# Six o tiles, weight buffers over both attention halves, and h differences made with h, in a windowed-attention encoder layer

## The chip, the cores and the metric

The kernel runs on one core of a Trainium2 chip. The metric is the time of one execution on the device, in microseconds (us). The core has five engines that run their own instruction queues in order: PE (TensorE, the matrix products), DVE (VectorE), ACT (ScalarE), POOL (GpSimd) and SP (SyncE, which here only issues DMAs). They wait for each other by semaphores.

## The reference

One layer of an encoder: windowed grouped-query attention, then a SwiGLU feed-forward, each between two RMSNorms with adaLN shift, scale and gate taken from a conditioning vector c. There are 2048 tokens of width 1024, 16 query heads over 4 key/value heads of width 64, a hidden width of 2816, all in fp32.

```
c_act = silu(c)
mod = c_act @ ada_w + ada_b                       # 6 x 1024
sh1, sc1, g1, sh2, sc2, g2 = split(mod, 6)
h = rmsnorm(x, mix_norm_pre) * (1 + sc1) + sh1
y = windowed_gqa_sink(h, w_qkv, w_o, sink, bias)  # blocks of 128 queries against 384 keys
x = x + g1 * rmsnorm(y, mix_norm_post)
h = rmsnorm(x, ffn_norm_pre) * (1 + sc2) + sh2
y = (silu(h @ w_in_a) * (h @ w_in_b)) @ w_out
x = x + g2 * rmsnorm(y, ffn_norm_post)
```

## The kernel before

**Products.** Every large product is done as three matmuls (`three`, L144 to L148): each operand is split into a high and a low part (`split`, L150 to L152: ACT casts the high part, DVE or POOL subtracts it to get the low part), and hi*hi, hi*lo and lo*hi are summed in one PSUM bank. A tile of 128x512 results over 1024 inputs takes 24 matmuls of 512 columns.

**Chunks and units.** The 2048 tokens are four chunks c of 512. Chunks 0 and 1 get their q, k and v first. Then 64 attention units follow, one for each chunk, key/value head g and block of 128 queries. A unit (L408) is named by its block b = 4c+jb and by g: `s8_0_3` is the score product of block 8, key/value head 0, fourth query head. A unit has eight score matmuls (L430), a DVE reduction with the bias (L435), exponentials on ACT (L437), a scaling on POOL (L443); two units later come its transposes (`t`, L453), their split, the products with v (`o`, L458 and L459) and the store of the result to `o_d` (L467).

**Fillers.** Between two units `Budget.pull` lets a generator write a few matmuls of other work into PE's queue: 19 a unit in the first 32 units, 20 in the second (`FILL`). In the first half these are q, k and v of chunks 2 and 3 (tiles `psq2_n`, `psq3_n`, 24 tiles of 24 matmuls). In the second half they are the output projection (`OProj`, L515): eight tiles `py{c}_{n}` a chunk, each from the four attention results `ol{c}_{g}` (L526, split by POOL, for chunk 3 by DVE) and a weight tile `wo{c}_{n}` (for chunks 0 and 3 loaded raw as `wor` at L537 and split; chunk 0 writes its split weights to `wo_d`, chunks 1 and 2 load them, L542). The last six `py` tiles of chunk 2 are held until the scores of the last unit are queued. `psF`, two PSUM banks, is shared by the `py` tiles and by the small sums `nst` of the norms.

**Ends.** `ends` (L569) follows a chunk's `py` tiles: the sum of squares `nsto` (two matmuls), the residual x1 on POOL (L505, L506, stored to `x1_d`), the second sum `nstx`, and `make_h2` (L497 to L500: a POOL multiplication, an ACT scale and shift, a store to `h2_d`). Chunk 1's `make_h2` comes last of these, after the final attention units. Chunk 3's projection (`py3_n`) follows by itself, with its own pools. For chunks 2 and 3 norm, residual and h are made later, inside the feed-forward (`late_residuals`, one step per block).

**Feed-forward.** It works on halves hf of 1024 tokens. A block (L731) forms two by two output tiles from seven products of sums and differences of operands, 84 matmuls of 512 columns (`pc0_u` to `pc6_u`). The token operands are h of two chunks (`b11`, `b21`, `b22`) and four differences (`t1` to `t4`); the seven weight operands are made and split by DVE for each block (`ws`, `wa`, L752 to L760). For hf 0 the h tiles are loaded back from `h2_d` as `fx` (L881), 12 for `b11` and `t2` and 16 for the rest; the differences are made on the spot: DVE at L887 and L888, and in `differences` POOL at L705 and L710 and DVE at L706 and L712. For hf 1 they are loaded ready-made from `hd_d`.

**adaLN.** The 48 columns `mod` are 48 DVE reductions of a 128x1024 weight tile `ada` against the broadcast silu(c) (L260), spread over the projection and attention phases; tiles 40 to 47 give the gate g2, used only in the last norm.

**Order.** The program is written in one order and a scheduler sorts each engine's queue by its own model when it is built; the queues are fixed from then on. Buffers come from pools stacked from the left or the right end of the on-chip memory: a pool opened in the place of an older one waits for the last use of the tiles that lay there.

## Time and profile before

| what | us |
|---|---|
| median of 3 runs (lowest to highest) | 2191.41 (2188.45 to 2195.57) |
| the profiled execution | 2197.15 |
| its span in the profile | 2195.3 |
| busy in it: PE / DVE / ACT / POOL | 2072.1 / 1668.4 / 1080.6 / 774.2 |

The profile is of one execution. A row of the page's groups reads: line, engine, operation, the tile written and those read, shape, count, then busy time and mean nanoseconds of one, and last how long the engine had idled just before these instructions and which engine, tile and line ended that. A row of the table of windows gives for a stretch of time each engine's busy time and number of instructions, PE's granted clock as a share of the full one, and the DMA engines' share and rate. A busy PE is not always a fast one, since a matmul that runs at a lower clock counts as busy for longer; the number of matmuls in a window tells more.

### The profile page before, as it was taken

How to read it: one execution, taken by the hardware profiler on the slowest of the kernel's cores; microseconds unless marked ns; L12 is line 12 of the kernel's file. 1: busy time of each engine (PE TensorE's matmuls, PEld its weight loads, DVE VectorE, ACT ScalarE, POOL GpSimd, SP SyncE). 2: the span in 40 equal slices, each digit the busy share in tenths (PEclk: the TensorE clock that was granted, in tenths of full speed). 3: DMA queues.
4: the chain of work that ended last, by engine and by line, in shares of the span. 5: the costliest groups of instructions: out<-in, count | busy, mean ns of one | idle time of the engine just before them, and what ended most of it. 6: DMA issues, size and time to landing. Idle time of an engine off the chain costs nothing. (4 is left out here: it accounts for less than half of the span.)

```text
span 2195.3 us, 28935 instructions
## 1 busy us (share of the span) xinstructions
PE 2072.1 (94%) x9366; PEld 1677.9 (76%) x9366; DVE 1668.4 (76%) x2917; ACT 1080.6 (49%) x2125; POOL 774.2 (35%) x695
## 2 busy tenths in 40 slices
PE   6998999989989998899999989999999999998997
PEld 4786878767777776778888868888888788877886
DVE  8657676676766579877888797766664788999987
ACT  4546565677757664443434353333332654465432
POOL 3403333355696865434344522222221000220040
PEclk8998999999999999999999999999999999999998
DMA  8786665576865683444445663223231544348442
GB/s 287 252 272 225 189 195 166 167 232 213 301 222 204 202 311 129 152 163 153 161 156 180 220 226 110 107 101 115 101 105 41 205 149 148 127 152 278 158 130 101
DMA packets 195764, 390.05 MB, mean 178 GB/s; under 512 B 19563, under 2 KB 61596, under 8 KB 190492
## 3 DMA queue, kind: packets, MB, share of 16 engines
q1 hardware_dynamic: 195036, 387.68, 53.0%
q8 instruction: 74, 1.21, 0.2%
q14 instruction: 78, 0.64, 0.1%
q10 hardware_dynamic: 576, 0.52, 0.1%
HBM read 268.55 MB, written 119.57 MB: 177 GB/s over the span
## 5 line engine op out<-in xcount | busy, mean ns | idle before, releaser
L435 DVE CUSTOM_DVE_ANT_0 pr<-s,bias,nsink 128x384 f32<-128x384 f32 (+1 forms) x256 | 149.1, 595 | 121.6 <-PE s L430 100.0
L147 PE MATMUL pc_i<-ht,ws_i 128*128 128x512 f32 x528 | 207.2, 392 | 1.0 <-DVE ht L152 1.0
L146 PE MATMUL pc_i<-ht,ws_i 128*128 128x512 f32 x528 | 207.5, 393 | 0.6 <-DVE u_i L813 0.6
L148 PE MATMUL pc_i<-ht,ws_i 128*128 128x512 f32 x528 | 207.0, 392 | 0.0
L823 POOL TENSOR_TENSOR p_i<-p_i,u_i 128x512 f32<-128x512 f32 x44 | 80.0, 1818 | 326.8 <-DVE u_i L810 180.9
L437 ACT ACTIVATE pr<-pr,nm 128x385 f32<-128x385 f32 (+1 forms) x256 | 154.0, 605 | 72.3 <-DVE nm L435 64.2
L958 POOL TENSOR_TENSOR z<-z,z 128x512 f32<-128x512 f32 x32 | 53.8, 1696 | 358.6 <-DVE z L954 338.4
L443 POOL TENSOR_SCALAR pr<-pr,rs 128x384 f32<-128x384 f32 (+1 forms) x256 | 146.3, 591 | 92.4 <-DVE rs L441 90.5
L430 PE MATMUL s<-k,q 128*128 128x384 f32 (+1 forms) x512 | 138.9, 368 | 23.4 <-DVE nm L435 15.7
L151 ACT CAST ws_i<-s_i 128x512 fp32r<-128x512 f32 x132 | 81.5, 619 | 128.4 <-PE pc_i L148 122.3
L146 PE MATMUL pc_i<-hb,wa_i 128*128 128x512 f32 x352 | 139.3, 396 | 0.6 <-DVE b_i L807 0.6
L151 ACT CAST wa_i<-wiri 128x512 fp32r<-128x512 f32 x132 | 81.9, 620 | 117.2 <-PE pc_i L148 111.1
L148 PE MATMUL pc_i<-hb,wa_i 128*128 128x512 f32 x352 | 138.9, 395 | 0.0
L147 PE MATMUL pc_i<-hb,wa_i 128*128 128x512 f32 x352 | 138.8, 394 | 0.0
L152 DVE TENSOR_TENSOR plo<-t,phi 128x512 fp32r<-128x512 f32 x184 | 121.7, 683 | 13.2 <-ACT phi L151 12.3
L430 PEld LDWEIGHTS s<-k,q 128*128 128x128 f32 x512 | 89.7, 200 | 46.8 <-DVE nm L435 29.9
L146 PEld LDWEIGHTS pc_i<-ht,ws_i 128*128 128x128 f32 x528 | 99.3, 188 | 24.4 <-issue 1.0
L147 PEld LDWEIGHTS pc_i<-ht,ws_i 128*128 128x128 f32 x528 | 99.2, 188 | 23.7 <-DVE ht L152 1.5
L453 PE MATMUL t<-ident,pr 128*128 128x128 f32 x736 | 114.0, 281 | 2.5 <-DVE plo L152 2.3
L148 PEld LDWEIGHTS pc_i<-ht,ws_i 128*128 128x128 f32 x528 | 99.2, 188 | 22.2
L152 DVE TENSOR_TENSOR ws_i<-s_i,ws_i 128x512 fp32r<-128x512 f32 x132 | 107.7, 816 | 5.0 <-ACT ws_i L151 4.7
L152 DVE TENSOR_TENSOR wa_i<-wiri,wa_i 128x512 fp32r<-128x512 f32 x132 | 106.1, 804 | 5.6 <-ACT wa_i L151 5.3
(323 smaller groups left out, 6200.3 us busy)
## 6 DMA issues: line engine op xcount, KB each, us to landing
wiri<-w_in SPq DMA_DIRECT2D x88, 512.0 KB, 4.7
ada<-ada_w SPq DMA_DIRECT2D x48, 512.0 KB, 5.5
wiro<-w_out SPq DMA_DIRECT2D x48, 384.0 KB, 3.8
q_d<-e SPq DMA_DIRECT2D x64, 256.0 KB, 4.1
q<-q_d SPq DMA_DIRECT2D x16, 1024.0 KB, 5.5
wo<-wo_d SPq DMA_DIRECT2D x16, 1024.0 KB, 6.0
g_d_b<-p_i SPq DMA_DIRECT2D x44, 256.0 KB, 4.8
g_d_t<-p_i SPq DMA_DIRECT2D x40, 256.0 KB, 2.0
```

The costliest lines, as they stand in the source:

```text
L146: pe.matmul(ps, w[0], h[0], start=first, stop=False)
L147: pe.matmul(ps, w[0], h[1], start=False, stop=False)
L148: pe.matmul(ps, w[1], h[0], start=False, stop=last)
L151: act.copy(hi, src)
L152: return eng.tensor_tensor(lo, src, f(hi), ALU.subtract).ins
L430: m = pe.matmul(ps[:, :n], q[:, h, jb * P:(jb + 1) * P], kk[:, i, (jb + j0) * P:(jb + j1) * P], start=i == 0, stop=i == 1)
L435: red = dve.tensor_tensor_reduce(pr[:, h, :n], ps[:, :n], bias[g][:, h, j0 * P:j1 * P], -1.0, nsink[:, hh:hh + 1], ALU.add, ALU.min, nm[:, ...
L437: act.activation(pr[:, h, :n + 1], pr[:, h, :n + 1], AF.Exp, bias=nm[:, h:h + 1], scale=-1.0, accum_out=rs[:, h:h + 1])
L443: pool.tensor_scalar(pr[:, h, :n], pr[:, h, :n], rs[:, h:h + 1], 1.0, ALU.mult, ALU.mult)
L453: pe.transpose(pt[:, h * P:(h + 1) * P], pr[:, h, jj * P:(jj + 1) * P], ident)
L823: pool.tensor_tensor(sa, sa, b, ALU.mult)
L958: (pool if (i, x) in ((2, 2), (4, 4), (5, 5), (6, 6)) else dve).tensor_tensor(sums[hf, n2, x], sums[hf, n2, x], sums[hf, n2, y], ALU.add)
```

## The change

It has five parts.

1. **Fillers**: 18 instead of 19 matmuls a unit in the first half.
2. **Pools**: the x tiles `xs` and the norm's scratch `nrm` now lie at the bottom of their stack, below the h tiles. The projection's attention results get six buffers instead of four, opened where `xs` lay. The weight pool `ws` of the first half stays open and serves the projection's weights too, with two split buffers instead of three and two raw ones instead of one for chunk 0; the y tiles get 12 buffers instead of 14.
3. **adaLN**: tiles 40 to 47 leave the second half of attention, with the second copy of silu(c). They are done in the feed-forward as 16 reductions of half the width (`late_ada`), one per block after the late residuals, into hf 1.
4. **Chunk 1's h**: made in pairs of tiles. With each pair the two tiles of chunk 0's h are loaded back (`hf`), and the differences t1 to t4 are made by DVE and stored to a second `hd_d`. The residual's filler steps are four tiles each instead of three.
5. **Feed-forward start**: all 28 operands are loaded ready from `h2_d` and `hd_d` into their final place and only split there; the 16 DVE and 8 POOL differences on `fx` are gone.

```diff
@@ -44,12 +44,14 @@
-FILL = (19, 20)
+FILL = (18, 20)
-ADA_UNITS = (range(1, 32, 2), range(34, 52, 2))
+ADA_UNITS = range(1, 32, 2)
+OBUFS = 6
@@ -153,10 +156,10 @@
+    xs = open_pool(com, "xs", 8)
+    nrm = open_pool(com, "nrm")
     hs = open_pool(com, "hs", 2 * KT)
     ev = open_pool(com, "ev", 2)
-    nrm = open_pool(com, "nrm")
-    xs = open_pool(com, "xs", 8)
@@ -373,7 +375,7 @@
-    ws = open_pool(com, "ws", 2)
+    wop = ws = open_pool(att, "ws", 2, side="right")
@@ -512,6 +514,20 @@
+    def differences(b11, b12, b21, b22, give, engs=(pool, dve)):
...
@@ -523,7 +539,7 @@
-                t = op.tile([P, 2, 2, CH], F32R, tag="o", name=f"ol{c}_{g}", bufs=4)
+                t = op.tile([P, 2, 2, CH], F32R, tag="o", name=f"ol{c}_{g}", bufs=4 if c == NCH - 1 else OBUFS)
@@ -531,9 +547,9 @@
-                w = wop.tile([P, 2, KT, P], F32R, tag="w", name=f"wo{c}_{n}", bufs=2 if c == NCH - 1 else 3)
+                w = wop.tile([P, 2, KT, P], F32R, tag="w", name=f"wo{c}_{n}", bufs=2)
-                    raw = wop.tile([P, KT, P], F32, tag="raw", name=f"wor{c}_{n}", bufs=3 if c else 1)
+                    raw = wop.tile([P, KT, P], F32, tag="raw", name=f"wor{c}_{n}", bufs=3 if c else 2)
@@ -550,7 +566,7 @@
-                y = yp.tile([P, CH], F32, tag="y", name=f"y{c}_{n}", bufs=4 if c == NCH - 1 else 14)
+                y = yp.tile([P, CH], F32, tag="y", name=f"y{c}_{n}", bufs=4 if c == NCH - 1 else 12)
@@ -580,14 +596,19 @@
             for k in range(KT):
                 residual(c, k, self.ys[k], yp.tile([P, CH], F32, tag="xr", name=f"xr{c}_{k}", bufs=3), r,
-                if k % 3 == 2:
+                if k % 4 == 3:
-            yield
             for k in range(KT):
                 make_h2(self.ys[k], c, k, r)
-                if k % 3 == 2:
+                if k % 2:
+                    if c == CPH - 1:
+                        first = [yp.tile([P, CH], F32, tag="xr", name=f"hf{j}", bufs=3) for j in (k - 1, k)]
+                        for j in range(2):
+                            sp.dma_start(first[j], h2_d[c - 1][:, k - 1 + j, :])
+                        differences(first[0], self.ys[k - 1], first[1], self.ys[k],
+                                    lambda n, t: sp.dma_start(hd_d[0][k // 2][n], t) if n[0] == "t" else None, (dve, dve))
@@ -620,30 +641,23 @@
-    ada_units = [*ADA_UNITS[0], *ADA_UNITS[1]]
-    HALF_ADA = len(ADA_UNITS[0]) - 1
-    late = list(range(2 * KT + ADA_A, 6 * KT))
+    late = list(range(2 * KT + ADA_A, 5 * KT))
-    op = wop = yp = None
+    op = yp = None
         if i == half:
-            assert not waiting
+            assert not waiting and not late
             dve.tensor_tensor(coef[:, 1, :], mod[:, 16:24], gains[:, 1, :], ALU.mult)
             com.close()
+            op = open_pool(oend, "op", OBUFS)
-            cb = yp.tile([P, D], F32, tag="cb", name="cb2")
-            sp.dma_start(cb, cb_d)
-            cbs.append(cb)
-            wop = open_pool(oend, "wop", 2)
-            op = open_pool(oend, "op", 4)
@@ -653,11 +667,11 @@
-        if i in ada_units:
+        if i in ADA_UNITS:
-            waiting = [ada_load(late.pop(0), ws if i < half else yp)] if i != ada_units[HALF_ADA] and late else []
+            waiting = [ada_load(late.pop(0), ws)] if late else []
@@ -665,8 +679,6 @@
-    assert not late and not waiting
-    dve.tensor_tensor(coef[:, 3, :], mod[:, 40:48], gains[:, 3, :], ALU.mult)
@@ -686,31 +698,14 @@
+    wi = [open_pool(early, "wi0"), None]
     hA = open_pool(early, "hA", KT // 2)
-    wi = [open_pool(early, "wi0"), None]
...
@@ -864,51 +856,47 @@
-                                lambda n, t: sp.dma_start(hd_d[k // 2][n], t) if n[0] == "t" else None)
+                                lambda n, t: sp.dma_start(hd_d[1][k // 2][n], t) if n[0] == "t" else None)
-    late = late_residuals()
+    def late_ada():
+        for i in range(2):
+            cols = slice(i * CH, (i + 1) * CH)
+            cb = temp(f"cb{i}", "r", 2)
+            sp.dma_start(cb, cb_d[:, cols])
+            for t in range(5 * KT, 6 * KT):
+                w = temp(f"ada{t}_{i}", "r", 2)
+                sp.dma_start(w, a["ada_w"][t][:, cols])
+                yield
+                dve.tensor_tensor_reduce(w, w, cb, 1.0, (mod if i else adab)[:, t:t + 1], ALU.mult, ALU.add, mod[:, t:t + 1])
+        dve.tensor_tensor(coef[:, 3, :], mod[:, 40:48], gains[:, 3, :], ALU.mult)
+    late = chain(late_residuals(), late_ada())
-    st0 = ExitStack()
-    tmp0 = open_pool(st0, "tmp0", 10)
-    half = Operands("0", K2, None)
-    def h_blocks(k, names, st):
-        b = []
-        for n in names:
-            b.append(temp0(f"fx{k}_{n}_{st}"))
-            sp.dma_start(b[-1], h2_d[int(n[2]) - 1][:, 2 * k + (n[1] == "2"), :])
-        return b
+    half = Operands("0", K2, lambda n, k: hd_d[0][k][n] if n[0] == "t" else
+                    h2_d[int(n[2]) - 1][:, 2 * k + (n[1] == "2"), :])
     with tc.high_priority(offset=1):
-        for k in range(K2):
-            b11, t1, t2 = h_blocks(k, ("b11", "b12", "b22"), 0)
-            dve.tensor_tensor(t1, t1, b11, ALU.subtract)
-            dve.tensor_tensor(t2, t2, t1, ALU.subtract)
-            half.put("b11", k, b11)
-            half.put("t2", k, t2)
+        half.load("b11", "t2")
     lasto.close()
     wi[1] = open_pool(ffn, "wi1", side="right")
     with tc.high_priority(offset=100):
-        for k in range(K2):
-            differences(*h_blocks(k, ("b11", "b12", "b21", "b22"), 1),
-                        lambda n, t: half.put(n, k, t) if n not in ("b11", "t2") else None)
-    st0.close()
+        half.load(*[n for n in OPERANDS if n not in ("b11", "t2")])
     for hf in range(S // HALF):
                 hid.step(i)
-            if hf == 0:
-                next(late, None)
+            next(late, None)
-            half = Operands("1", K2, lambda n, k: hd_d[k][n] if n[0] == "t" else
+            half = Operands("1", K2, lambda n, k: hd_d[1][k][n] if n[0] == "t" else
+    assert next(late, None) is None
         hid.step(i)
```

The number of PE instructions is the same. On DVE the differences are 16 again, in another place, and eight reductions become 16 of half width; POOL has eight instructions fewer, the differences it made on `fx`. SP issues 33 more DMAs: eight loads `hf`, 16 stores to the second `hd_d`, eight more half `ada` loads, one for silu(c).

How the queues move, at the three places that the prediction speaks of. First PE where the second half of attention starts. Before, from the third score product of block 11, head 0:

```order
L459 MATMUL o7_3_5060<-plo7_3_2_5089,v1_3_4174 128x512
L453 MATMUL t8_0_2_5185<-ident_343,pr8_0_4907 128x128 x4
L430 MATMUL s11_0_1_5241<-k2_0_4577,q2_0_4575 128x384 x2
L146 MATMUL py0_0_5009<-ol0_0_4986,wo0_0_5003 128x512
L147 MATMUL py0_0_5009<-ol0_0_4986,wo0_0_5003 128x512
```

After, at the same tile `py0_0`:

```order
L432 MATMUL s8_0_3_4936<-k2_0_4546,q2_0_4544 128x384 x2
L455 MATMUL t7_3_0_5071<-ident_359,pr7_3_4812 128x128
L455 MATMUL t7_3_1_5082<-ident_359,pr7_3_4812 128x128
L149 MATMUL py0_0_5019<-ol0_0_4996,wo0_0_5013 128x512
L149 MATMUL py0_1_5122<-ol0_0_4996,wo0_1_5116 128x512
```

The first projection tile stands behind the scores of block 8 instead of block 11, three units earlier; the q, k, v tiles, which before ended two units before the half, now reach into its last unit.

Second, PE between chunk 1's projection tiles, where no filler is queued. Before (the rows left out are of the same units):

```order
L146 MATMUL py1_4_6526<-ol1_0_5941,wo1_4_6524 128x512
...
L430 MATMUL s15_0_0_6969<-k3_0_6202,q3_0_6200 128x256 x2
L430 MATMUL s12_1_0_7090<-k3_1_6683,q3_1_6681 128x384 x2
L430 MATMUL s13_1_0_7207<-k3_1_6683,q3_1_6681 128x384 x2
L430 MATMUL s14_1_0_7309<-k3_1_6683,q3_1_6681 128x384 x2
L128 MATMUL nstx0_6626<-nhix0_6627,ones_342 128x512
L146 MATMUL py1_5_6642<-ol1_0_5941,wo1_5_6640 128x512
```

After:

```order
L149 MATMUL py1_3_6415<-ol1_3_5952,wo1_3_6413 128x512
...
L432 MATMUL s10_3_0_6438<-k2_3_5776,q2_3_5774 128x384 x2
L432 MATMUL s11_3_0_6548<-k2_3_5776,q2_3_5774 128x384 x2
L432 MATMUL s12_0_0_6652<-k3_0_6198,q3_0_6196 128x384 x2
L432 MATMUL s13_0_0_6764<-k3_0_6198,q3_0_6196 128x384 x2
L432 MATMUL s14_0_0_6851<-k3_0_6198,q3_0_6196 128x384 x2
L432 MATMUL s15_0_0_6955<-k3_0_6198,q3_0_6196 128x256 x2
L131 MATMUL nstx0_6515<-nhix0_6516,ones_358 128x512
L149 MATMUL py1_4_6531<-ol1_0_5940,wo1_4_6529 128x512
```

The stretch without fillers, which ends behind `nstx0` in both, was four units long and is six now. Between `py2_1` and `py2_2`, where chunk 2's tiles are held, six units go without fillers in both.

Third, SP before the last projection `py3`. Before:

```order
L467 DMA o_d3_3_123<-of14_3_8037 256x1x128
L527 DMA ol3_0_8347<-o_d3_0_120 128x1024
L527 DMA ol3_1_8351<-o_d3_1_121 128x1024
L527 DMA ol3_2_8355<-o_d3_2_122 128x1024
L537 DMA wor3_0_8365<-w_o 128x1024
L467 DMA o_d3_3_123<-of15_3_8066 256x1x128
L563 DMA y_d0_324<-y2_5_8228 128x512
L537 DMA wor3_1_8399<-w_o 128x1024
L537 DMA wor3_2_8435<-w_o 128x1024
L500 DMA h2_d1_321<-y1_0_6057 128x512
L527 DMA ol3_3_8359<-o_d3_3_123 128x1024
```

After:

```order
L502 DMA h2_d1_337<-y1_3_6509 128x512
L543 DMA ol3_0_8380<-o_d3_0_120 128x1024
L558 DMA wo2_7_8307<-wo_d7_351 128x2048
L469 DMA o_d3_3_123<-of15_3_8060 256x1x128
...
L502 DMA h2_d1_337<-y1_7_7023 128x512
L579 DMA y_d0_340<-y2_6_8283 128x512
L543 DMA ol3_1_8384<-o_d3_1_121 128x1024
L543 DMA ol3_2_8388<-o_d3_2_122 128x1024
L553 DMA wor3_0_8398<-w_o 128x1024
L543 DMA ol3_3_8392<-o_d3_3_123 128x1024
```

The loads of chunk 3's first three attention results and of its first weight tile stood ahead of the stores of chunk 1's h; now three of the four and the weight stand behind all eight of these stores and behind the store of `y2_6`, and the last weight tile of chunk 2 behind the fourth of them. On DVE, after, twelve of the sixteen differences stand among the splits of `ol3`: the seven rows ahead of the last splits that `py3_0` needs are

```order
L521 TENSOR_TENSOR hf4_8295<-y1_4_6625,hf4_8295 128x512
L522 TENSOR_TENSOR y1_4_6625<-y1_5_6740,y1_4_6625 128x512
L526 TENSOR_TENSOR y1_5_6740<-y1_5_6740,hf4_8295 128x512
L155 TENSOR_TENSOR ol3_1_8384<-ol3_1_8384 128x1024
L155 TENSOR_TENSOR ol3_2_8388<-ol3_2_8388 128x1024
L155 TENSOR_TENSOR wo3_0_8397<-wor3_0_8398,wo3_0_8397 128x1024
L155 TENSOR_TENSOR ol3_3_8392<-ol3_3_8392 128x1024
```

so the difference of the sixth tile of chunk 1's h (`y1_5`) comes ahead of them, where before no row of h stood there.

33 lines of the change are left out of this document (14 added, 19 removed).

## The prediction

> **What bounds the kernel now.** I read the page's head and the chain that ended last, then the table of windows around the places the change touches, then PE's groups in the stretches where it loses time.
>
> ```profile
> span 2195.3 us, 28935 instructions
> PE 2072.1 (94%) x9366; PEld 1677.9 (76%) x9366; DVE 1668.4 (76%) x2917; ACT 1080.6 (49%) x2125; POOL 774.2 (35%) x695
> PE 36%; DVE 4%; DMA 2%; issue 1%; ACT 1%; POOL 0%; SPq 0%; DVEq 0%; POOLq 0%; ACTq 0%
> ...
> 484.00:584.00 100.00, 94.81 (x473) 77.07 (x474) 67.15 (x170) 68.33 (x158) 58.31 (x74) 0.98 0.73 251
> 735.00:786.00 51.00, 46.90 (x220) 37.72 (x219) 27.10 (x45) 33.89 (x70) 38.34 (x38) 0.97 0.76 237
> 786.00:814.00 28.00, 27.00 (x118) 21.98 (x118) 19.99 (x23) 19.89 (x31) 18.23 (x9) 1.00 1.04 383
> 814.00:838.00 24.00, 22.84 (x100) 18.56 (x100) 23.92 (x29) 14.11 (x26) 16.98 (x6) 1.00 0.47 166
> 838.00:862.00 24.00, 17.20 (x63) 12.32 (x62) 23.70 (x28) 12.02 (x22) 11.66 (x8) 0.93 0.34 109
> 862.00:880.00 18.00, 17.02 (x74) 13.40 (x72) 17.20 (x30) 8.05 (x14) 8.67 (x1) 1.00 0.35 132
> 1265.00:1310.00 45.00, 39.35 (x162) 30.35 (x161) 44.98 (x67) 25.62 (x48) 10.04 (x6) 0.96 0.69 248
> 1310.00:1700.00 390.00, 390.00 (x1690) 318.13 (x1690) 261.78 (x379) 118.53 (x198) 88.75 (x59) 1.00 0.27 96
> ```
>
> PE is busy 94% of the span and carries most of the chain. The change leaves its instructions alone, so it can only win back time in which PE waits or runs slowly. The last row gives PE's pace with nothing in its way: 1690 matmuls of 512 columns in 390 us, 0.231 us each, DVE at two thirds. In 814 to 862, where chunk 3's projection ends and the first feed-forward block runs, DVE is busy 47.6 of 48 us, while PE gets through 63 matmuls in the last 24 us instead of some 104. There DVE is the bound. Attention is of a third kind: nobody is full, and PE loses time unit by unit.
>
> **Attention.** PE's groups in 450 to 488, which ends where the projection has properly begun, then in 632 to 662 between chunk 1's projection tiles, and a row that prices transposes:
>
> ```profile
> L430 PE MATMUL s<-k,q 128*128 128x384 f32 x56 | 16.3, 383 | 4.2 <-DVE nm L435 3.9
> L453 PE MATMUL t<-ident,pr 128*128 128x128 f32 x68 | 12.0, 292 | 0.1
> L458 PE MATMUL o<-phi,v 128*128 128x512 f32 x17 | 7.5, 441 | 1.1 <-ACT phi L151 0.8 <-issue 0.2
> L459 PE MATMUL o<-plo,v 128*128 128x512 f32 x16 | 7.3, 456 | 0.2 <-DVE plo L152 0.2
> ...
> L453 PE MATMUL t<-ident,pr 128*128 128x128 f32 x52 | 8.9, 285 | 0.1
> L430 PE MATMUL s<-k,q 128*128 128x384 f32 x26 | 7.4, 392 | 5.7 <-DVE nm L435 5.7
> L459 PE MATMUL o<-plo,v 128*128 128x512 f32 x12 | 5.8, 480 | 0.0
> L458 PE MATMUL o<-phi,v 128*128 128x512 f32 x12 | 5.7, 478 | 0.4 <-DVE of L466 0.2
> L430 PE MATMUL s<-k,q 128*128 128x256 f32 x8 | 2.5, 438 | 0.3 <-DVE nm L435 0.3
> ...
> 481.42 0.60 PE L453 MATMUL t<-ident,pr 128*128 128x128 f32 x4
> ```
>
> Four transposes in a row end 0.60 us after the first began, one alone takes 0.28: 0.107 us each. By columns a score matmul of 384 is 0.173. The first stretch holds 56 x 0.173 + 68 x 0.107 + 33 x 0.231 (and three filler matmuls, 0.7) = 25.3 us of work in 38: 12.7 lost in seven units (56 scores by eight), 1.8 each. The second holds 17.9 us (six further matmuls among it) in 30: 12.1 lost in 4.25 units, 2.85 each. In 484 to 584 fillers are dense: a unit of 26 matmuls is 4.05 us of work, 20 fillers 4.62; 473 matmuls are 10.3 such units, 89 us of work in 100, 1.05 lost a unit. So a unit without fillers costs 0.75 to 1.8 us more than one with them.
>
> The number of fillers is fixed; early ones are missing later. In the first half 576 filler matmuls at 18 instead of 19 a unit last 32 units instead of 30.3: 1.7 units gained. In the second half the order puts `py0_0` three units earlier, the gap behind `nstx0` is two longer, the one ahead of `py2_2` unchanged: one unit. Together 2.7 units, 2.0 to 4.9 us. From the other side: if the 12.7 all went and two units at 2.85 came back, 7.0. Below, nothing: PE's queue is in order, and an early `py0_0` whose `ol` or `wo` is still in POOL's split holds up the scores behind it. I take **-4.5**. The nine `ada` reductions that leave (1.28 us each, row below) lay where DVE was busy 67 of 100: nothing.
>
> **The tail of attention.** The rows are PE's timeline, POOL's multiplications for chunk 1's h, and what the last projection must wait for: landing times, then casts and splits.
>
> ```profile
> 769.07 0.39 PE L129 MATMUL nstx<-nlox,ones 128*128 128x512 f32 x1
> ...
> 769.99 0.39 PE L148 MATMUL py<-ol,wo 128*128 128x512 f32 x1
> 773.24 0.50 PE L146 MATMUL py<-ol,wo 128*128 128x512 f32 x1 [2.87 <-ACT ysq L560]
> ...
> 785.67 0.39 PE L148 MATMUL py<-ol,wo 128*128 128x512 f32 x1
> 786.51 0.50 PE L146 MATMUL py<-ol,wo 128*128 128x512 f32 x1 [0.45 <-ACT ysq L560]
> ...
> L498 POOL TENSOR_TENSOR y<-y,nx x8: 1292/2224/2282, 775.6 to 789.2; 128x512 f32<-128x512 f32 x8
> ...
> wo<-wo_d SPq DMA_DIRECT2D x16, 1024.0 KB, 6.0
> ...
> ol<-o_d SPq DMA_DIRECT2D x4, 512.0 KB, 4.7
> ...
> L152 DVE TENSOR_TENSOR wo<-wor,wo 128x1024 fp32r<-128x1024 f32 x8 | 12.5, 1558 | 2.1 <-ACT wo L151 2.0
> L152 DVE TENSOR_TENSOR ol<-ol 128x1024 fp32r<-128x1024 f32 x4 | 7.5, 1905 | 4.2 <-ACT ol L151 4.2
> L151 ACT CAST wo<-wor 128x1024 fp32r<-128x1024 f32 x16 | 16.7, 1044 | 8.8 <-DMA wor<-w_o 8.7
> ```
>
> What may go: the pause before `py2_6` (773.24 less 770.22, 3.0) and its slow start, since two tiles took 12.7 us instead of 11.1 (1.6): -4.6. `py3_0` then followed with 0.45 us of idling.
>
> What comes: `wo2_7` is issued behind the store of `y1_3`. POOL's first multiplication began 6.5 us after `nstx1`; four of them at 1.29 to 2.28, about 1 for ACT and 6.0 to land make 18.7 to 22.6, and the turn of `py2_7`, three tiles after `nstx1` in the new order, is at 16.6: a wait of 2 to 6, I take +3. The loads of `ol3_1`, `ol3_2`, `wor3_0` and `ol3_3` stand behind the store of `y2_6`: 0.7 after `py2_6` for its copy (estimated as a 128x512 cast), some 1.5 for four issues, 4.7 to land, 1.0 to cast, 1.9 for the last split, 9.8 in all, against 5.5 of `py2_7` and its wait: 1.3 to 4.3, and 1.6 for a slow start as above. I take +5.5. Sum **+4**. Lower end: -4.6, if no load is late. Upper end: 24 stores and loads of 256 KB are new here, 6.3 MB, and
>
> ```profile
> DMA packets 7814, 17.17 MB, mean 264 GB/s; under 512 B 797, under 2 KB 2077, under 8 KB 7426
> ```
>
> is the rate in 735 to 800: 24 us if all of it went ahead of those loads. I stay near the lower half, because the order issues only about half of it ahead, and spread over three tiles.
>
> **The feed-forward's start.** The differences on `fx`, who waited for them, and block 1:
>
> ```profile
> L887 DVE TENSOR_TENSOR fx_b<-fx_b,fx_b x4: 678/686/1769, 791.5 to 806.4; 128x512 f32<-128x512 f32 x4
> L888 DVE TENSOR_TENSOR fx_b<-fx_b,fx_b x4: 678/686/694, 794.5 to 809.3; 128x512 f32<-128x512 f32 x4
> L706 DVE TENSOR_TENSOR fx_b<-fx_b,fx_b x4: 678/680/684, 824.9 to 852.2; 128x512 f32<-128x512 f32 x4
> L712 DVE TENSOR_TENSOR fx_b<-fx_b,fx_b x4: 679/1212/1772, 842.5 to 855.7; 128x512 f32<-128x512 f32 x4
> ...
> ACT ht L151 <- DVE fx_b L712: 9.0, 4, 4.1
> ...
> 884.97 0.80 PE L146 MATMUL pc_i<-hb,ws_i 128*128 128x512 f32 x1 [5.95 <-ACT p_i L794]
> ...
> L260 DVE CUSTOM_DVE_ANT_0 ada<-ada,cb,adab x48: 1272/1280/3514, 13.8 to 628.3; 128x1024 f32<-128x1024 f32 x48
> ```
>
> From 786 to 862 PE does 281 matmuls, 64.9 us of work in 76: 11.1 lost. The 16 differences cost DVE about 14 us there (four each at 0.95, 0.69, 0.68, 1.22), and the chain POOL, DVE, POOL, DVE made ACT wait 9.0 in front of the `t4` casts. Both leave. DVE's 67.6 us in these windows become 53.5, under PE's 64.9, and the number of loads (28) stays. At most 11.1 comes back; nothing, if splits of `ol3` and `wo3`, later now by the wait above, slide into it. I take **-8**. Block 1 lost 0.9 in 862 to 880 (18.0 less 74 x 0.231) and then 5.95 behind the same overfull DVE: **-4** of 6.8, between 0 and that.
>
> **adaLN later.** A half reduction is 0.64 us by the last row. Five stand, in the new order, ahead of hf 1's last operand splits, where DVE has no idle time (1265 to 1310: 44.98 of 45): 3.2 us. Eight weight operations of a later block, which stood there before, stand behind: I take 0, between -3 and +3.2. The eleven others fall into DVE's third of idle time (1310 to 1700); without that cover they would cost 7.
>
> **Sum**: -4.5 + 4 - 8 - 4 = -12.5, so 2197.15 becomes 2184.65 for an execution like the profiled one. That one lies 5.74 above the median of the runs shown; on the median's scale 2178.9, **2179 us**.
>
> **The rivals.**
> *More gain* (0.12): no load late at the tail, all that is lost is won. -7 - 4.6 - 11 - 6.8 = -29, 2162. For it: `py3_0` was nearly on time before. Against: the queue of SP.
> *The gain is eaten* (0.24): fillers only change places (0), both tail waits at their long ends (+10), block 0 gets half of its gain back (-6), block 1 -4. Zero, 2191; with two thirds of the waits 2188. For it: a fixed number of fillers.
> *Slower* (0.15), by one mechanism: DVE and POOL hold each other up. The fx rows have 0.68 and 1.77 us for one operation, POOL's row 1.29 and 2.28. Sixteen differences at 1.77 are 28 us instead of 11, while POOL multiplies `y1` at 2.28; `y1_5` comes 6.5 + 13.7 + 1 after `nstx1`, its two differences 3.5 later, and the four splits ahead of `py3_0` (7.3) behind those in DVE's queue: 32 us, against four tiles, 22.2. That is +9.8 and 1.6 of slow start instead of the +5.5, and 17 us more for DVE eat both feed-forward terms: -4.5 - 4.6 + 3 + 11.4 = +5.3; with another 2 for later `wo3` splits, 2199. It decides once the pairs really alternate; in the old trace only some did. The Trainium skill, "SBUF — State Buffer" (Who interferes with whom), has this as a rule: a DVE instruction with two inputs in SBUF and a GpSimd instruction that reads SBUF exclude each other, and the later one blocks until the first is through. By that rule moving differences beside POOL's multiplications would always cost; the trace agrees with the slow values, but its means lie in between, so it gets 0.15.
> *The reductions at hf 1's start cost* (0.07): all 3.2 and a DVE backlog for two blocks, +6, 2185.
>
> **How the numbers follow.** The forecast keeps 0.42, with a range of its own of 2172 to 2186. A measurement of this kernel can tell about 0.3%, 6.6 us, from no change, so faster means under 2184.8. The forecast gives 0.37 to faster, more gain 0.12, the two middle rivals 0.08: 0.57. No change: 0.05 + 0.2 + 0.03 = 0.28. Slower: 0.15. The range, from just above "more gain" to just under "slower", is 2163 to 2197.
>
> **What would show it.** Right: PE's matmuls dense from the scores of block 8 on; the stretch behind `nstx0` about 5 us per unit for six units; 786 to 862's DVE under 90% with no `fx` rows, and the first block's end 8 us closer to `py3_0`. A gap ahead of `py3_0`, released by DVE's `ol` split, of 2 to 6 us. Wrong: `y1` differences near 1.77 us, a gap there above 10, or PE idle at `py0_0` and `py0_1` behind POOL's splits.

## The result

| | us, median (lowest to highest) |
|---|---|
| before | 2191.05 (2188.45 to 2195.57), 4 runs |
| changed | 2166.02 (2165.77 to 2166.94), 4 runs |
| ratio | 0.9884, 95% interval 0.9867 to 0.9901 |

The change takes 25.0 us off, where my sum had 12.5. The four runs lie within 1.2 us; the four of before span 7, and 23 on a later chip 14.5 (2183.74 to 2198.26).

The head of the changed kernel's page, and its windows from the start of the second half of attention on. The edges: 463 `s8_0_0`, 715 `s15_3_0`, 774 `py3_0`, 860 the end of block 1, 1250 a place within the last two blocks of hf 0 (they begin at 1218), 1299 block 2 of hf 1.

```profile
span 2164.3 us, 28995 instructions
PE 2055.8 (95%) x9366; PEld 1666.6 (77%) x9366; DVE 1649.8 (76%) x2933; ACT 1076.4 (50%) x2125; POOL 737.5 (34%) x687
...
715.00:774.00 59.00, 47.53 (x221) 38.03 (x220) 32.05 (x56) 35.45 (x65) 32.80 (x34) 0.94 0.69 233
774.00:821.00 47.00, 46.81 (x192) 38.03 (x193) 35.26 (x46) 28.50 (x47) 13.27 (x6) 0.93 0.96 349
821.00:860.00 39.00, 39.00 (x171) 31.90 (x170) 37.93 (x56) 26.93 (x44) 13.90 (x7) 1.00 0.56 192
860.00:1250.00 390.00, 384.30 (x1658) 312.36 (x1657) 316.98 (x425) 155.95 (x261) 163.77 (x109) 0.99 0.54 180
1250.00:1299.00 49.00, 46.53 (x199) 36.79 (x198) 49.00 (x77) 20.93 (x39) 12.69 (x9) 1.00 0.59 201
1299.00:1689.00 390.00, 388.27 (x1686) 316.03 (x1686) 267.42 (x403) 118.09 (x206) 87.41 (x59) 1.00 0.31 106
```

From `py3_0` to the end of block 1 PE now does 363 matmuls in 86 us, 0.237 us each, close to its full pace; before, the same work took about 104 us. DVE still fills 821 to 860 (37.9 of 39), but PE no longer waits for it. The tail, 715 to 774, has become longer: the same 221 matmuls, 59 us instead of 52.

For a comparison stretch by stretch I sort every PE instruction by its name and count what it takes at full pace (0.2275 us for 512 columns, in proportion for 384 and 256, 0.109 for a transpose); the rest of a stretch is *lost*. Since the execution in before's first trace took 5.7 us more than the median, I took a second trace, a run that I tell of below, and set that beside the change. The stretches: start up to the first score; the two halves of attention; the tail from `s15_3_0` to `py3_0`; from there to the end of block 1; the rest of hf 0 up to its last pair of blocks; the turn to hf 1, two blocks deep; hf 1; the output products.

```
us lost           start half1 half2  tail py3-b1  hf0  turn  hf1   out
before, first      48.4  29.9  53.5   7.8   21.3 10.1   9.7  4.3  31.7
before, second     48.4  27.6  47.3   7.9   22.8  6.2   8.6  4.3  33.7
changed            50.8  27.1  34.4  14.9    3.6 13.3   4.1  6.7  30.8
changed, second    49.0  26.9  35.1  15.0    3.7 11.9   6.2  6.7  31.0
pools alone        48.1  26.4  44.7   7.6   22.2 12.6   9.4  4.3  31.8
adaLN alone        50.0  28.5  42.3   3.0   20.5  9.4   6.2  6.7  32.5
h diff. alone      48.7  29.1  44.2  14.4    6.9 11.8   4.7  4.3  30.0
pools and adaLN    47.6  26.8  36.3   9.3   23.7  9.1   6.3  6.0  34.5
```

Second trace against second trace: attention -12.2 in its second half and -0.7 in its first, the tail +7.1, the feed-forward's start -19.1, the rest of hf 0 +5.7, the turn -2.4, hf 1 +2.4, the output -2.7. With +0.6 at the start this is about 21 us between two single executions; the 25.0 are between medians. Two traces of one kernel differ by up to 6 us in a stretch, as the first two rows show, so differences of a few us in single rows say little.

### The profile page after: what moved, and what is told of

It reads as the page before. It is cut to its first block, busy times and chain, and to the rows that moved or that the text cites. A ratio compares the mean times of both kernels' runs of the same rounds, so it can differ in the third digit from the quotient of the medians.

```text
span 2164.3 us, 28995 instructions
## 1 busy us (share of the span) xinstructions
PE 2055.8 (95%) x9366; PEld 1666.6 (77%) x9366; DVE 1649.8 (76%) x2933; ACT 1076.4 (50%) x2125; POOL 737.5 (34%) x687
## 5 line engine op out<-in xcount | busy, mean ns | idle before, releaser
L815 POOL TENSOR_TENSOR p_i<-p_i,u_i 128x512 f32<-128x512 f32 x44 | 71.5, 1625 | 310.7 <-DVE u_i L802 153.6
L149 PE MATMUL py<-ol,wo 128*128 128x512 f32 x256 | 103.3, 405 | 11.9 <-ACT wo L154 7.4
L155 DVE TENSOR_TENSOR ws_i<-s_i,ws_i 128x512 fp32r<-128x512 f32 x132 | 104.6, 792 | 10.9 <-ACT ws_i L154 10.7
```

The source lines that it names most:

```text
L149: pe.matmul(ps, w[0], h[0], start=first, stop=False)
L155: return eng.tensor_tensor(lo, src, f(hi), ALU.subtract).ins
L815: pool.tensor_tensor(sa, sa, b, ALU.mult)
```

## The parts alone

Each of the three large parts was put into the kernel before by itself. A change in one place makes the scheduler sort the queues anew, so most of these kernels also differ from before in the order of places that the edit does not touch. Theory 1 was that attention's gain, which already the first pair of traces showed to be far over my 4.5 us, comes from the order (fillers three units earlier). Theory 2 was that it comes from DVE, where the adaLN reductions no longer stand between the scores.

**The pools, the fillers and the four-tile steps of the residual.**

```diff
-FILL = (19, 20)
+FILL = (18, 20)
+OBUFS = 6
+    xs = open_pool(com, "xs", 8)          # below hs, as in the change
-    ws = open_pool(com, "ws", 2)
+    wop = ws = open_pool(att, "ws", 2, side="right")
...
```

> The kernel before with the fillers, the pools and the residual's four-tile steps of the change alone; adaLN tiles and h differences stay where they were. Theory 1 (the attention gain comes from fillers that start three units earlier): the second half of attention loses some 15 to 20 us less, time about 2173. Theory 2 (it comes from DVE, whose adaLN reductions and the small multiplication of gains held up the scores): the gain here is what I predicted for the order, 4 to 7 us, time about 2185.

Measured: 2187.88, ratio 0.9975 (0.9960 to 0.9990), 5.5 us. Half 2 loses 44.7, 2.6 less than before's second trace, and half 1 1.2 less. That is near the 4.5 I had predicted for the order, and no larger than what two traces of one kernel differ by; by the time, theory 1 falls as the explanation of the rest.

**adaLN late.**

```diff
-ADA_UNITS = (range(1, 32, 2), range(34, 52, 2))
+ADA_UNITS = range(1, 32, 2)
+    late = chain(late_residuals(), late_ada())
...
```

> The kernel before with the adaLN part alone: tiles 40 to 47 as half reductions in the feed-forward, none in the second half of attention. Theory 1: within 3 us of before, about 2190. Theory 2: the scores no longer wait behind reductions that last 2.07 us on average and behind a multiplication of 128x8 that lasted 7.33 us; 8 to 12 us faster, about 2181.

Measured: 2179.87, ratio 0.9950 (0.9928 to 0.9971), 11 us, as theory 2 expected. (The expectations and my prediction say nine reductions; the trace of before has eight in the second half.) By the traces 5 us of this lie in half 2 and another 5 in the tail, which loses 3.0 instead of 7.9.

**Only the small multiplication of gains moved.**

```diff
-    dve.tensor_tensor(coef[:, 3, :], mod[:, 40:48], gains[:, 3, :], ALU.mult)
     att.close()
...
+    dve.tensor_tensor(coef[:, 3, :], mod[:, 40:48], gains[:, 3, :], ALU.mult)
     hid = Hidden(half, HT - 1, hf)
```

> The kernel before with one instruction moved: the multiplication coef<-mod,gains of 128x8, which took 7.33 us on DVE among the last units of attention, now stands before the last feed-forward block. Theory 2 in its narrow form: PE's gap of 4.79 us behind it goes, 4 to 5 us faster, about 2186. Theory 1: no change, since the next wait takes its place.

Measured: 2191.74, ratio 1.0002 (0.9981 to 1.0023): no change. One instruction that lasts 7.3 us looked like an easy culprit; taking it away wins nothing that can be measured. This edit leaves PE's queue in half 2 as it was, instruction for instruction, and half 2 loses 46.4 in its trace.

**The h differences alone** (with the four-tile steps, which the same generator needs).

```diff
+                    if c == CPH - 1:
+                        first = [... name=f"hf{j}", bufs=3) for j in (k - 1, k)]
+                        differences(first[0], self.ys[k - 1], first[1], self.ys[k], ..., (dve, dve))
...
+        half.load("b11", "t2")
```

> The kernel before with the h differences alone (made with chunk 1's h, feed-forward operands loaded ready). Both theories: from py3_0 to the end of block 1 some 18 us less are lost, the tail of attention before py3_0 loses 7 more: 11 us faster, about 2180. If the 18 us need the other parts too (DVE free at that time), less than 6.

Measured: 2176.74, ratio 0.9926 (0.9901 to 0.9951), 16 us: the largest part. `py3_0` to the end of block 1 falls from 22.8 to 6.9 without help from the others, and the tail rises from 7.9 to 14.4. That is 9.4 net, near the 11 expected; the other some 6 us of the 16 stand in no one place of the trace (3 in half 2, 4 each in the turn and the output, against losses elsewhere).

**Pools and adaLN together**, without the differences.

> The kernel before with the pools and the adaLN part together, h differences where they were. If the two need each other in attention (dense fillers only pay when DVE has no reductions that POOL can hold up), the second half of attention loses 34 to 36 us as in the changed kernel, 10 us below either alone, and the time is about 2176 to 2178. If they only add, 2191 - 5.5 - 11 = 2175 with some 40 lost there; if the gain of attention is the differences' doing, about 2180 and 42.

Measured: 2182.00, ratio 0.9963 (0.9946 to 0.9980), 8 us. In half 2 the first branch holds: 36.3, against 44.7 and 42.3 alone, and PE's queue there is the changed kernel's, instruction for instruction (34.4 and 35.1); the h differences have no part in it. But the tail loses 9.3 where adaLN alone had 3.0, so the time is above the expected 2176 to 2178, and by the times the two together win no more than adaLN alone (0.9950, with overlapping intervals). Alone, the three parts win 5.5, 11 and 16, 33 in sum; together 25. By the traces the tail holds most of the overlap: adaLN's 5 us there do not survive once the loads come late.

**The two kernels again.** No edit in either.

> The kernel before, unchanged, for a second trace of it. In the traces of its relatives that share its order of attention, the second half of attention loses 44 to 46 us, not 53.5. If the first trace was an unlucky execution, this one shows 44 to 47 and no DVE instruction of over 4 us there; if 53.5 is usual, the multiplication of 128x8 again lasts several us.

Measured: 2188.35, ratio to the other runs of before 0.9991 (0.9969 to 1.0014). Half 2 loses 47.3, so 6 of the 53.5 were that execution's. The multiplication, however, lasts 7.3 us again, as in the second branch: a long multiplication and an unlucky execution are two things. In this trace the adaLN tiles' and the gains' rows in 440 to 740 are:

```profile
L260 DVE CUSTOM_DVE_ANT_0 ada<-ada,cb,adab x10: 1279/1754/3452, 443.5 to 621.9; 128x1024 f32<-128x1024 f32 x10
...
L669 DVE TENSOR_TENSOR coef<-mod,gains x1: 7335/7335/7335, 626.5 to 626.5; 128x8 f32<-128x8 f32 x1
```

> The changed kernel, unchanged, beside the other kernels of this call. 2166 as on the first chip, within 3 us; the second half of attention loses 34 to 36 us.

Measured: 2164.75, ratio 0.9885 (0.9852 to 0.9919), 35.1 lost in half 2.

## What the adaLN operations cost attention

**Twice as many.**

```diff
                     ada_reduce(*w)
+                    if i > half:
+                        ada_reduce(*w)
```

> The kernel before with each of the nine adaLN reductions of the second half of attention done twice in a row (the second on the product of the first, so the gate g2 is not the reference's). Taking the nine away alone won 11 to 12 us. If each costs the scores its own time on DVE (theory 2), nine more cost 9 to 12 us: about 2202. If only their presence in the order mattered, or the loads of the weight tiles, the time stays within 3 us of before.

Measured: 2196.72, ratio 1.0013 (0.9996 to 1.0030), 3 us. (The second reduction works on the first one's product, so this kernel's g2 is not the reference's.) Eight reductions more cost a quarter of what eight less win. The first branch fails; the second, within 3 us, is where the ratio lies, though its interval reaches to 6.6. Half 2 loses 44.7 in this trace, no more than before. By this run attention does not pay simply for the reductions' time on DVE. But PE's queue there has moved too: chunk 0's last projection tile starts 12 units into the half, where before it started 13.75 units into it. The order is a rival that this run leaves open.

The trace of the pools alone shows what can happen to one of them. POOL's timeline from 571 to 583 us, and below it DVE's (start, duration, engine, line, operation, output and input):

```profile
571.27 6.30 POOL L506 TENSOR_TENSOR y<-y,no 128x512 f32<-128x512 f32 x5
577.53 2.39 POOL L153 TENSOR_TENSOR ol<-ol 128x1024 fp32r<-128x1024 f32 x1
579.88 1.29 POOL L507 TENSOR_TENSOR y<-y,xr 128x512 f32<-128x512 f32 x1
581.15 1.18 POOL L427 TENSOR_SCALAR pr<-nsink 128x4 f32<-128x4 f32 x1
```

```profile
575.53 6.74 DVE L261 CUSTOM_DVE_ANT_0 ada<-ada,cb,adab 128x1024 f32<-128x1024 f32 x1
582.20 0.07 DVE L261 DVE_READ_ACCUMULATOR2_ANT mod<- 128x1 f32 x1
```

A reduction whose shortest of the eight takes 1.28 us lasts 6.74 here, while POOL goes from one instruction to the next without a gap, and it ends as POOL's last one here does. The 7.33 us of 128x8 stand beside POOL's back-to-back residual in the same way. By the Trainium skill, "SBUF — State Buffer" (Who interferes with whom), a DVE instruction with two inputs in SBUF and a GpSimd instruction that reads SBUF exclude each other for one instruction; the trace agrees, and here DVE seems to be kept out over several of POOL's in a row. I had cited that rule for the tail, and not for the eight reductions that the change takes out of attention.

To tell the exclusion from the time and from the loads, three kernels put something else at the reductions' places. All have the pools part, and compute the real reductions late, as the change does. Each has one of the three lines added.

```diff
-                    ada_reduce(*w)
+                    dve.tensor_tensor(w[1], w[1], cbs[-1], ALU.mult)          # two inputs
+                    dve.tensor_scalar(w[1], w[1], 1.0, 1.0, ALU.mult, ALU.mult)   # one input
+                    act.activation(w[1][:, :1], w[1][:, :1], AF.Copy)         # loads only
```

> The kernel before with the pools part, and the adaLN reductions computed late as in the change; but at the old places in the second half of attention DVE multiplies each loaded weight tile with silu(c) (two inputs in on-chip memory, 128x1024, result unused). This is the reductions' load and shape without their purpose. Both theories: like the pools part alone, 44 to 46 us lost in the second half of attention, against 36 when they are gone; the eight operations last between 1.2 and several us.

> The same with a multiplication by 1.0 in place (one input in on-chip memory, 128x1024). If POOL holds up only operations with two such inputs, these eight last the same short time each, none over 2 us, and the second half of attention loses 36 to 39 us, close to the kernel without them. If it is DVE's time or the weight tiles' loads, 43 to 46 us are lost as with two inputs.

> As the run with one input, but DVE does nothing with the eight weight tiles in the second half of attention; ACT touches one column of each, so the loads and buffers stay. If DVE's eight operations are what attention pays for, 36 to 39 us are lost in its second half, as without the adaLN part, and the time is about 2183; if the loads are, 43 to 46 us as before and about 2191.

| at the eight places | us | ratio to before | lost in half 2 |
|---|---|---|---|
| two inputs | 2196.34 | 1.0024 (1.0013 to 1.0035) | 48.9 |
| one input | 2191.93 | 1.0003 (0.9991 to 1.0016) | 44.5 |
| loads only | 2186.74 | 0.9970 (0.9957 to 0.9983) | 43.2 |
| nothing (pools and adaLN) | 2182.00 | 0.9963 (0.9946 to 0.9980) | 36.3 |
| the real reductions (pools alone) | 2187.88 | 0.9975 (0.9960 to 0.9990) | 44.7 |

By the ratios, leaving the two-input operation for a one-input one wins 4.6 us (the intervals just overlap), leaving that for loads only 7.2, and leaving the loads 1.5 with intervals that overlap. So an operation put on DVE at these places is not free: the two-input ones cost 11.8 us against loads only, 1.5 each. But the last row, with the real reductions, does not stand where the first does. The two-input kernel is 10.7 us slower than it, though it was meant to cost attention the same; 4.2 of that lie in half 2, and 4.7 in hf 1, where the late reductions are new. Against pools alone, loads only win nothing, and taking everything out wins 2.6 us with intervals that overlap. So these steps price the stand-ins, and not the reductions.

None of the three is a clean control either. The one-input operation is not spared as I expected; in its trace, the eight together (shortest, median and longest in ns), then one of them in DVE's timeline, then PE's (in brackets the wait ahead and what ended it),

```profile
L658 DVE TENSOR_SCALAR ada<-ada x8: 895/1105/5383, 492.8 to 623.4; 128x1024 f32<-128x1024 f32 x8
```

```profile
603.33 5.38 DVE L658 TENSOR_SCALAR ada<-ada 128x1024 f32<-128x1024 f32 x1
```

```profile
609.30 1.01 PE L431 MATMUL s<-k,q 128*128 128x384 f32 x2 [5.22 <-DVE nm L436]
```

one of the eight lasts 5.38 us (the shortest of them 0.895) and PE waits 5.22 behind the score reduction that follows it. POOL is busy without a gap up to 608.16 there, and the operation ends 0.55 us later. The Trainium skill, "SBUF — State Buffer" (Who interferes with whom), says that `tensor_scalar` can run in a two-port mode, and then contends with GpSimd too; the 5.38 us agrees. Here one sees the price directly: what DVE is held up on, the scores wait for.

With loads only, ACT touches the tiles, and it waits for their landing: its rows (shortest, median and longest in ns), and its idle time ahead of them (us, times) with what ended it, are

```profile
L658 ACT ACTIVATE ada<-ada x8: 202/203/236, 491.3 to 554.0; 128x1 f32<-128x1 f32 x8
  DMA ada<-ada_w: 10.8, 4
```

10.8 us in all, up to 4.9 at once, in the queue that also does the exponentials. The reductions and both DVE stand-ins never waited for a load. So the 43.2 of that trace can be ACT's, and say nothing of what the loads alone cost. And the order was sorted anew for each: PE's queue in half 2 is another in pools alone, in each of the three and in pools and adaLN.

What is shown is that the adaLN part by itself takes 11 us off, and that in half 2 the traces without DVE's eight operations and without ACT's touches lie at 34 to 42 us lost, those with them at 43 to 54. How much of it is DVE's time, POOL's exclusion, the loads or the order stays open.

## The tail, and what comes back later

The changed kernel's PE timeline ahead of `py2_7` and `py3_0`:

```profile
755.40 0.40 PE L151 MATMUL py<-ol,wo 128*128 128x512 f32 x1
759.39 0.47 PE L149 MATMUL py<-ol,wo 128*128 128x512 f32 x1 [3.60 <-DMA wo<-wo_d]
...
766.37 0.40 PE L151 MATMUL py<-ol,wo 128*128 128x512 f32 x1
774.15 0.80 PE L149 MATMUL py<-ol,wo 128*128 128x512 f32 x1 [7.38 <-ACT wo L154]
774.75 0.63 PE L150 MATMUL py<-ol,wo 128*128 128x512 f32 x1
```

Both predicted waits are there: 3.6 for the load of `wo2_7` and 7.4 ahead of `py3_0`, and then matmuls at little more than a third of the pace. The second is ended by ACT's cast of `py3_0`'s weight tile, the third cast in a row behind the late loads, and not by DVE's split of `ol3` as the prediction had it. SP issued those loads 9 to 11 us after `py2_6` ended (755.8):

```profile
764.35 0.41 SPq L579 DMA_DIRECT2D y_d<-y  x1
764.81 1.66 SPq L543 DMA_DIRECT2D ol<-o_d  x2
766.52 0.49 SPq L553 DMA_DIRECT2D wor<-w_o  x1
767.06 0.50 SPq L543 DMA_DIRECT2D ol<-o_d  x1
```

**The loads moved up.**

```diff
-                sp.dma_start(f(t[:, 1]), o_d[c][g])
+                with tc.high_priority(offset=200) if c == NCH - 1 else ExitStack():
+                    sp.dma_start(f(t[:, 1]), o_d[c][g])
...
```

> The changed kernel with one thing more: the loads and splits of chunk 3's attention results, of its first three weight tiles and of chunk 2's last three weight tiles get a higher priority in the order, so that on SP they stand ahead of most stores of chunk 1's h. The tail of attention lost 14.9 us in the changed kernel (4.0 ahead of py2_7, 7.8 ahead of py3_0, and slow starts). If the place in SP's queue is the cause, 6 to 9 us faster than the changed kernel, about 2158 to 2160; if the DMA engines' fill or POOL's multiplications are, within 3 us of it.

Measured: 2167.94, ratio 0.9887 (0.9865 to 0.9910): no change, where 6 to 9 us were expected. The tail loses 7.5 instead of 14.9, so SP's order is the cause of that half; but `py3_0` to block 1 loses 9.3 instead of 3.6, in rows like these, the first two behind the cast and the split of chunk 3's last results:

```profile
774.45 0.73 PE L150 MATMUL py<-ol,wo 128*128 128x512 f32 x2 [1.51 <-ACT ol L155]
775.71 0.50 PE L151 MATMUL py<-ol,wo 128*128 128x512 f32 x1 [0.53 <-DVE ol L156]
780.83 0.55 PE L150 MATMUL py<-ol,wo 128*128 128x512 f32 x1 [2.56 <-ACT yacc L577]
```

The load of `ol3_3`, which needs the last unit's result, was issued at 766.5, and ACT had idled 7.38 us for it when it began that cast, DVE 6.03 when it began the split.

**A third weight buffer**, the same priorities for chunk 3's loads, and the adaLN half reductions spread.

```diff
+            wx = open_pool(oend, "wx", 1)
...
+            with tc.issue_after(hid.mark) if hf else ExitStack():
+                next(late, None)
```

> The changed kernel with three edits: a third buffer for chunk 0's to 2's weight tiles, loads of chunk 3's attention results and first weight tiles at a higher priority, and the half reductions of the adaLN tiles tied behind a block's last DVE operation, so that they spread over 16 blocks. If wo2_7 and the place in SP's queue make the tail's waits, the tail loses under 5 us instead of 14.9; if the reductions in a bunch cost hf 1 its 2.4 to 4.4 us, hf 1 loses 4.3 again. Together 8 to 12 us faster than the changed kernel, about 2155 to 2158; if the last projection only waits later for ol3_3, 3 us faster, 2163.

Measured: 2163.45, ratio 0.9879 (0.9846 to 0.9911), 1.3 us under the changed kernel on the same chip, where 3 were expected in the lesser case. The tail loses 0.9, nothing more is to be had there; `py3_0` to block 1 loses 13.8. What the tail gives up is taken back within 90 us. Part of it is the load of `ol3_3` again, issued at 766.7: PE waits 1.60 for its cast, ACT having idled 8.04 for the load. That the rest comes because the same DVE has to do the differences, the splits for `py3` and the first block's operands either way is my reading, and not shown.

**Two more edits on that**: the last units' values at a higher priority, the late residual's norm one block later.

```diff
-                if k % 2:
+                if k in (3, 5, 7):
                     yield
+            yield
```

> The changed kernel with the three edits of the third weight buffer's run, and two more: the last two attention units at a higher priority, so that the store of block 15's result and the load of ol3_3 move ahead of h differences, and the norm of the late residuals one block later in the feed-forward. PE waited 4.0 to 5.2 us ahead of that norm's sum (nstl2) in the changed kernel. If the projection of chunk 3 starts clean: 9 us less lost between py3_0 and the end of block 1 than in the third weight buffer's run (13.8), and 4 less in hf 0: about 2152. If the waits only move on: 2160 to 2164.

Measured: 2173.67, ratio 0.9924 (0.9899 to 0.9949), slower than the changed kernel by some 8 us. `nstl2`'s wait is gone, but others of 4.3 and 4.8 us appear at the ends of later blocks, and the first block waits 4.9 and 4.7 us for its operands. The wait ahead of that norm's sum in the changed kernel is

```profile
942.83 0.79 PE L131 MATMUL nstl<-nhil,ones 128*128 128x512 f32 x1 [4.05 <-DVE nhil L129]
```

and 0.77 in before's second trace. So 3.3 of the 5.7 us more in hf 0 are this one place; the rest is no more than what two traces of one kernel differ by there. That the blocks come earlier and denser while the chain of the late residual (loads, POOL, DVE, ACT) does not is my reading of it.

## The smaller sizes

**19 fillers again in the first half; four o buffers.** Both on the changed kernel.

```diff
-FILL = (18, 20)
+FILL = (19, 20)
```

> The changed kernel with 19 filler matmuls a unit in the first half, as before. Theory 1 gives up the fillers in units 30 to 32: 3 to 5 us slower than the changed kernel, about 2170. If the earlier start of the projection comes from the pools alone: within 2 us, 2166.

Measured: 2175.06, ratio 0.9922 (0.9898 to 0.9946), 8 to 9 us slower, more than either branch. The traces do not place it: the first half loses 29.8 instead of 27.1, but other kernels with 18 fillers and the same PE queue in that half lose up to 29.1 there too; the rest lies in hf 0, the turn and hf 1, places where nothing was edited. PE's queue in the second half was sorted anew.

```diff
-OBUFS = 6
+OBUFS = 4
```

> The changed kernel with four buffers for attention results instead of six. The order starts py0_0 at the same place with four. If only the place of the pools matters: 2166 within 2 us; if the two more buffers let chunk 1's results be split ahead: 3 to 6 us slower, about 2170.

Measured: 2177.69, ratio 0.9923 (0.9895 to 0.9951). Half 2 loses 39.2 instead of 35, though `py0_0` starts at the same place, and `py3_0` to block 1 10.4 instead of 3.7. So the two more buffers do work, in part through the order: chunk 1's second tile starts 12.5 units into the half with four, 11.0 with six.

**The half reductions spread**, one a block, on the changed kernel.

> The changed kernel with the half reductions tied behind a block's last DVE operation, one a block over 16 blocks of hf 1, nothing else. hf 1 lost 4.3 us without these reductions, 6.7 with them in a bunch, and 4.3 spread out in the run with the third weight buffer: 2 to 3 us faster than the changed kernel, about 2163. If the bunch is not what costs: within 1 us, 2165 to 2166.

Measured: 2161.90 (2157.55 to 2163.15), ratio 0.9855 (0.9829 to 0.9881): the fastest of all these kernels, 3 to 4 us under the changed one's medians, though the intervals of the two ratios overlap. The trace is plain: PE's queue is the changed kernel's throughout, and hf 1 loses 4.3, as before the change, instead of 6.7. The reductions in the changed kernel, then spread:

```profile
L872 DVE CUSTOM_DVE_ANT_0 ada<-ada,cb,adab x8: 740/751/1783, 1228.4 to 1292.8; 128x512 f32<-128x512 f32 x8
L872 DVE CUSTOM_DVE_ANT_0 ada<-ada,cb,mod x8: 737/753/1784, 1301.3 to 1334.0; 128x512 f32<-128x512 f32 x8
```

```profile
L872 DVE CUSTOM_DVE_ANT_0 ada<-ada,cb,adab x8: 737/741/744, 1303.6 to 1434.4; 128x512 f32<-128x512 f32 x8
L872 DVE CUSTOM_DVE_ANT_0 ada<-ada,cb,mod x8: 741/744/744, 1453.7 to 1588.7; 128x512 f32<-128x512 f32 x8
```

## Where the prediction was right and wrong

The direction was right and the time lies inside the range, but the size is off by two. By its own terms:

- **Attention, -4.5.** Measured -12.9 (-0.7 and -12.2). The term for the order was right in size: the pools alone win 2.6 in half 2 and 1.2 in half 1 by the traces, 5.5 by the time. What 18 instead of 19 fillers win in the first half is too little to be read from single traces (some 26 to 29 us lost with 18, 28 to 30 with 19). The step that failed is the sentence that the reductions "lay where DVE was busy 67 of 100: nothing". The runs showed 11 us for the adaLN part alone, and 8.4 in half 2 where it joins the pools. A share of busy time does not say what an operation holds up. The price in that sentence was short as well: 1.28 us is the median of all 48 rows, while the eight of the second half took

```profile
L260 DVE CUSTOM_DVE_ANT_0 ada<-ada,cb,adab x8: 1280/1848/3514, 495.1 to 628.3; 128x1024 f32<-128x1024 f32 x8
```

  17.3 us together, 2.2 each, and up to 6.74 in a relative. Why their going wins as much as it does stays open, as said above. The unit price of a stretch without fillers, 2.85 us, came from a stretch that held the wait of 4.8 us behind the gains' multiplication; without that wait it is 1.7 by the same working.
- **The tail, +4.** Measured +7.1, by SP's order and `wo2_7` as named: 3.6 and 7.4 us of waiting where I took 3 and up to 4.3. The pause ahead of `py2_6` did go, down to 0.64 us. Within its bounds, sized low: the sum let SP issue the loads within some 2 us of `py2_6`, and they were issued 9 to 11 us after it, since SP issued DMAs of h and its differences first, 0.3 to 1.3 us each.
- **The feed-forward's start, -8 and -4.** Measured -19.1 of 22.8, and -15.9 with the h differences alone. The mechanism was right: the 16 differences and their chain through POOL were the bound. The term was sized low: I kept back 6 of 18 for splits of `ol3` and `wo3` that would slide into the first block, and they did not. In the changed kernel's trace the last split starts at 812.5 and the block's first product at 821.0:

```profile
L155 DVE TENSOR_TENSOR wo<-wor,wo x8: 1224/1388/1570, 774.1 to 812.5; 128x1024 fp32r<-128x1024 f32 x8
L149 PE MATMUL pc_i<-hb,wa_i x26: 389/389/398, 821.0 to 880.0; 128*128 128x512 f32 x26
```

- **adaLN later, 0.** Measured +2.4 in hf 1, where I let DVE's idle third hide them; in a bunch, some of them at 1.78 us, they did not hide, spread they do. The turn gained 2.4 by the second traces.
- **Not in the sum**: +5.7 in the rest of hf 0, 3.3 of it one wait.
- **The rivals.** "More gain" named the size, 2162, and the wrong reason: it had no load late at the tail, and the tail got worse. "Slower" by DVE and POOL did not decide the tail. The differences there lasted

```profile
L521 DVE TENSOR_TENSOR hf<-y,hf x4: 689/1028/1437, 744.7 to 790.6; 128x512 f32<-128x512 f32 x4
L522 DVE TENSOR_TENSOR y<-y,y x4: 691/720/1769, 751.3 to 792.4; 128x512 f32<-128x512 f32 x4
L526 DVE TENSOR_TENSOR y<-y,hf x4: 678/907/1666, 753.9 to 793.1; 128x512 f32<-128x512 f32 x4
L528 DVE TENSOR_TENSOR hf<-hf,y x4: 676/690/694, 756.7 to 794.8; 128x512 f32<-128x512 f32 x4
```

  0.68 to 1.77 us, with medians nearer the fast value than the slow. Whether the same mechanism decided in attention, where the change takes such operations away, is not shown.

## What to carry to other kernels

Price an operation that leaves a queue by how long it lasts in its own stretch and by what stands behind it in that queue, not by the busy share of its engine: eight reductions that I put at nothing were worth 11 us. Before trusting one trace, take a second of the same kernel: 6 us of the second half of attention, which I costed, belonged to that execution. Before crediting an edit with a stretch, see whether the queues there were sorted anew; only kernels with the same order compare one thing. A wait that is won at one place can come back a little later, as the tail's did.

## What was not expected of the hardware

- A DVE operation of 128x8 lasted 7.33 and 7.34 us in two traces, 0.2 to 0.4 in relatives of the kernel, beside an unbroken run of POOL instructions; a reduction 6.74 instead of 1.28; and an operation with a single input in on-chip memory 5.38 instead of about 1.
- The time's spread fell with the change: 23 runs of before span 14.5 us; ten runs each of the kernels with DVE operations on the weight tiles in the second half of attention 7 to 19; ten of pools and adaLN together 6, and of loads only 5; four each of the changed kernel 1.2 and 4. Fewer runs narrow a spread too, and that it goes with those operations is seen, not shown to be cause and effect.
